# Gate stage of a RetNet and gated-MLP step: low part of v by VectorE a step later, gating chain cut into steps

## The chip, the cores and the metric

The kernel runs as one program on one core of a Trainium2 chip. The metric is the device time of an execution in microseconds (us). An execution is measured from its launch to its end. The profile shows one execution by itself, from the first to the last instruction (its span).

The core has a matrix engine (TensorE, PE in the rows; its weight loads are listed as PEld), a vector engine (VectorE, DVE), an activation engine (ScalarE, ACT), a general engine (GpSimd, POOL) and a queue processor (SyncE, SP) that here only issues DMAs. Each engine works through its own queue in order. An instruction that waits holds back all that stand behind it in that queue.

## The reference, cut to what matters

The model has two layers over 1024 prompt rows and 8 single new tokens (T = 1032 columns together), model width 1024. Layer 0 is a retention mixer; layer 1 is the chunked gated MLP that the change touches:

```python
u, v, g = split(x @ w_in, 3)             # each 2048 wide
u = gelu(u); v = layer_norm(gelu(v), ln_g, ln_b)
ws = where(causal, w_s[:, :128, :128], 0)        # 8 groups, 128 x 128
mixed = einsum('gij,bcjgd->bcigd', ws, chunks(v)) + b_s
y = u * mixed * silu(g)
x = layer_norm(ALPHA * x + y @ w_out)
```

All is fp32. The kernel gets near-fp32 products out of TensorE by splitting each operand into a high part (a cast to fp32r) and a low part (the value less the high part) and adding three products: high x high, high x low, low x high (`mm3`).

## The kernel before, in words

**Stages.** Layer 0 fills the first 950 us or so. Then `x1_transpose` and its sums prepare layer 1's input, units `tm34`, `tm36`, `tm38` compute v, and sixteen units `fm40` to `fm55` (class `FmUnit`, number n = 0 to 15) compute u and g, 128 columns of each per unit. This last stretch, from about 1135 to 1540 us, is the gate stage. An output projection (`OutProj`) ends the kernel.

**One unit.** A unit computes a 2 x 2 block product in seven products (`p5, p1, p3, p6, p2, p7, p4`), each in two steps (two column halves, c = 0 and 1, of 258 columns), so a unit is 14 steps. The order is written out by hand: the unit's `p5` stands ahead of the previous unit's `p4`, so steps 0 and 1 of a unit are its own `p5`, steps 2 and 3 are `p4` of the unit before, then come `p1`, `p3`, `p6`, `p2`, `p7`. Products of one unit accumulate in the same PSUM banks: `p6` goes on top of `p1`, so it can start only when ACT has copied `p1` out (`act.copy(t, ps)`, L1189); `p7` waits until DVE has added `p6`'s sum (L1193); `p3` waits for the copy of `p5`. Results lie in two tiles of 128 x 1032 per unit, `u` and `s`.

**Around each step**, the loop over `seq` calls `hook(s)`, which runs what was put on the list `later` (`run_later`) and then the prepared weight parts of coming products (`prep`: high part by ACT, L1164; low part by DVE, L1036, or for `p3`, `p2`, `p7` by a negation on ACT, L1167, and an accumulating DMA from POOL, L1171). Then it calls `hook_c2` (the spatial part, below), then the unit's step with its matmuls and evacuations. What is put on `later` in one step is issued at the head of the next.

**The end of a unit.** After `p4`'s second half, `later` gets `out`: in the next step (step 4 of the following unit) ACT makes the gelu of half of `u` (L1200) and, for even n, the silu of all of `s` (L1202); a step later (step 5) DVE multiplies `u` by `s` (L1203). For odd n the silu of `s` (L1197) runs one step after `p7`.

**The spatial part.** Group g (0 to 7) covers the two units 40+2g and 41+2g. `s_load` fetches gelu(v) from DRAM in two halves (`lv`, 128 x 4 x 256) with gain, bias and spatial weights (`gbw`). `s_prep` normalizes it, one quarter of a half per call (L1340, L1341 on DVE); part 0 first masks and splits the weights (POOL L1329, ACT `wsh` L1333, DVE `wsl` L1334). After each fourth part the half is split: `vh` by ACT's cast (L1345), `vl` by ACT's negation (L1346) and POOL's accumulating DMA that adds `lv` to it (L1347). From group 2 on, parts 0 to 3 are called in steps 4, 6, 8 and 10 of an odd unit and parts 4 to 7 in steps 0, 2, 4 and 6 of the next; groups 0 and 1 are prepared earlier, in `fm40` to `fm42`. `s_mix` (twelve matmuls `mx`, six for each half, which need both `vh` and `vl` of that half) stands at step 2 of an odd unit, for group 0 at step 0 of `fm42`. `s_y` transposes the result (PE `yt`, L1371) and multiplies it by `u` (DVE `yy`, L1374) at step 7 of the following units; the very first stands at step 4 of `fm42`.

**Other work in the stage.** `vd_norm` (DVE L1287, L1288, then `md` L1294) normalizes the new tokens' v, at step 2 of `fm41` and of `fm44`; `vdg` and `vdb` are its gain and bias tiles.

**Buffers.** Nearly every tile (`wr`, `w_p`, `wt`, `u`, `s`, `lv`, `gbw`, `vh`, `vl`, `mx`, `yy`, `vdg`, `vdb`, the operands made from layer 1's input) is one of `S(...)`: they share one pool of 49 buffers (`NSLOT`). A buffer is given on when all uses of its old tile are over; the first writer of a new tile then waits for the last user of the old one, whatever that was.

Of the kernel before, what the change touches and what calls it, by code (L numbers as in the profile page):

```python
# [13 lines left out]
AF = mybir.ActivationFunctionType  # L14
ALU = mybir.AluOpType
# [6 lines left out]
T = SEQ + NB  # L22
# [12 lines left out]
HT = T // 2  # L35
# [6 lines left out]
def retnet_gmlp_step(ctx: ExitStack, tc: tile.TileContext, a, o):  # L42
    nc = tc.nc
    act, dve, pool, pe, sp = nc.scalar, nc.vector, nc.gpsimd, nc.tensor, nc.sync
# [8 lines left out]
    def S(name, shape=(128, T), dt=F32):  # L53
        return big.tile(list(shape), dt, tag="s", name=name)

    def PS(name):
        return psp.tile([128, 512], F32, tag="ps", name=name)

    def f(ap):
        return ap.bitcast(F32)  # L60
# [4 lines left out]
    def mm3(out, lh, ll, rh, rl, start, stop, skip=False):  # L65
        mm(out, lh, rh, start, False, skip)
        mm(out, lh, rl, False, False, skip)
        mm(out, ll, rh, False, stop, skip)
# [70 lines left out]
    later = []  # L139
# [655 lines left out]
    def x_op(key, kt, sl):  # L795

        hh, ll = X[key]
        return hh[kt // 2][:, kt % 2, sl], ll[kt // 2][:, kt % 2, sl]
# [239 lines left out]
    class TmUnit(Unit):  # L1038
# [30 lines left out]
        def step(self, k, i):  # L1069
            ch, first = BANK[k], k in self.FIRST  # L1070
            if first and i % 2 == 0:
                self.ps[ch, i // 2] = PS(f"tm{self.p}{ch}_{i // 2}")
            ps = self.ps[ch, i // 2]
            wh, wl = self.op[k]
            sl = slice(i * 128, i * 128 + 128)
            out = ps[:, (i % 2) * 256:(i % 2) * 256 + 256]
            for kt in range(4):
                ws = slice(kt * 256, kt * 256 + 256)
                mm3(out, *x_op(XKEY[k], kt, sl), wh[:, ws], wl[:, ws], first and kt == 0 and i % 2 == 0, kt == 3,
                    skip=not first or i % 2 == 1)  # L1080
            if i % 2:
                self.evac(k, i // 2, ps)
            if i == 3:
                self.dec(k)
# [49 lines left out]
    class FmUnit(Unit):  # L1134
# [38 lines left out]
        def step(self, k, c):  # L1173
            ch, first = BANK[k], k in self.FIRST
            if first:
                self.ps[ch, c] = PS(f"fm{self.p}{ch}_{c}")
            ps = self.ps[ch, c][:, :258]
            wh, wl = self.op[k]
            sl = slice(c * 258, c * 258 + 258)
            for kt in range(4):  # L1180
                ws = slice(kt * 128, kt * 128 + 128)
                mm3(ps, wh[:, ws], wl[:, ws], *x_op(XKEY[k], kt, sl), first and kt == 0, kt == 3, skip=not first)
            i, n = OUT[k]
            if k == "p5":
                if c == 0:
                    self.q = [S(f"{s}{self.n}") for s in "us"]
            t = self.q[n][:, i * HT + c * 258:i * HT + c * 258 + 258]
            if k in ("p5", "p1", "p3"):
                act.copy(t, ps)  # L1189
            elif k == "p4":  # L1190
                act.activation(t, ps, AF.Gelu)
            else:
                dve.tensor_tensor(t, t, ps, ALU.add)  # L1193
            if c == 1:
                u, s = self.q
                if k == "p7" and self.n % 2:
                    later.append(lambda: act.activation(s, s, AF.Silu))  # L1197
                if k == "p4":
                    def out():
                        act.activation(u[:, :HT], u[:, :HT], AF.Gelu)  # L1200
                        if self.n % 2 == 0:
                            act.activation(s, s, AF.Silu)  # L1202
                        later.append(lambda: dve.tensor_tensor(u, u, s, ALU.mult))  # L1203
                    later.append(out)

    X1_SUMS = {}
    for n, (key, part) in {10: ("s1", 0), 11: ("s1", 3), 13: ("s1", 2), 14: ("s1", 5), 15: ("s2", 0), 16: ("s2", 3),
# [114 lines left out]
    def s_prep(g, part):  # L1322

        if g >= GR:
            return
        q = G[g]
        if part == 0:
            wr = q["wr"]
            pool.affine_select(out=wr, in_=wr, pattern=[[1, 128]], compare_op=ALU.is_ge, fill=0.0, base=0,  # L1329
                               channel_multiplier=-1)  # L1330
            wh = small.tile([128, 128], F32R, tag="wsh", name=f"wsh{g}")
            wl = small.tile([128, 128], F32R, tag="wsl", name=f"wsl{g}")
            act.copy(wh, wr)  # L1333
            dve.tensor_tensor(wl, wr, f(wh), ALU.subtract)  # L1334
            q["w"] = (wh, wl)
            q["vhl"] = []
        half, k = divmod(part, 4)
        t = q["v"][half]
        tb = half * 4 + k
        dve.scalar_tensor_tensor(t[:, k, :], t[:, k, :], vmv[:, tb, 0:1], q["gt"], ALU.subtract, ALU.mult)  # L1340
        dve.scalar_tensor_tensor(t[:, k, :], t[:, k, :], vrs[:, tb:tb + 1], q["bt"], ALU.mult, ALU.add)  # L1341
        if k == 3:
            hh = S(f"vh{g}_{half}", (128, 4, 256), F32R)
            ll = S(f"vl{g}_{half}", (128, 4, 256), F32R)
            act.copy(hh, t)  # L1345
            act.mul(ll, t, -1.0)  # L1346
            pool.dma_start(ll, t, accum_op=ALU.add)  # L1347
            q["vhl"].append((hh, ll))

    def s_mix(g):  # L1350
# [45 lines left out]
    def hook_c2(fb, o):  # L1396
# [15 lines left out]
        if (fb, o) in PREP0:  # L1412
            s_prep(0, PREP0.index((fb, o)))
        if (fb, o) in PREP1:
            s_prep(1, PREP1.index((fb, o)))
        if g == 0:
            if (fb, o) == (1, 5):
                s_load(1)
        elif odd:
            if o == 0:  # L1420
                s_load(g + 1)
            if o == 2:
                s_mix(g)
            if o in (4, 6, 8, 10):
                s_prep(g + 1, (o - 4) // 2)
        elif g > 1 and o in (0, 2, 4, 6):
            s_prep(g, 4 + o // 2)
# [25 lines left out]
    for u, k in seq:  # L1453
        for i in range(u.STEPS):
            s = first[u, k] + i
# [95 lines left out]
```

## Time and profile before

| | us |
|---|---|
| median of 3 runs | 1748.51 (1746.86 to 1751.27) |
| profiled execution | 1749.73 |
| its span, first to last instruction | 1748.0 |
| granted TensorE clock, mean over the span | 0.987 of full |
| busy in the span: PE / DVE / ACT / POOL | 1692.2 / 900.0 / 664.9 / 407.5 |

Busy times are sums over instructions of one engine. An idle stretch of an engine is put down to what released the instruction behind it ("<-"). A matmul's row gives when it started and, in brackets, how long PE had been idle before.

### The profile page before, as it was taken

What the parts mean: (1) busy time and instruction counts of PE and PEld (TensorE: products, weight loads), DVE (VectorE), ACT (ScalarE), POOL (GpSimd) and SP (SyncE); (2) the same over time, 40 slices, a digit from 0 to 9 for tenths busy, and PEclk for the clock granted to TensorE, in tenths of its full rate; (3) what the DMA queues carried; (4) which work ended last, traced back from release to release, by engine and by line L of the source; (5) the groups of instructions that cost most, each with busy time, mean ns of one, the idle gap of its engine ahead of it and who ended that gap; (6) DMA issues with size and microseconds to landing.
All of it is one profiled execution on the core that took longest, in us unless ns stands there. A gap on an engine that the chain in (4) does not pass through costs nothing. (4 is left out here: it accounts for less than half of the span.)

```text
span 1748.0 us, 25438 instructions
## 1 busy us (share of the span) xinstructions
PE 1692.2 (97%) x10304; PEld 1511.5 (86%) x10304; DVE 900.0 (51%) x1446; ACT 664.9 (38%) x1043; POOL 407.5 (23%) x331
## 2 busy tenths in 40 slices
PE   9999999999999999999999999997899999999996
PEld 8898897979999887877778999996889999977775
DVE  7134453633331577753359574564465555543347
ACT  4122424234332454431205343344556666731102
POOL 4122231411110666531107100011111111231103
PEclk9999999999999999999999999998999999999998
DMA  7135555555532544341102312263655666692206
GB/s 266 72 122 191 183 204 187 212 165 209 217 145 93 197 157 157 133 181 49 49 25 110 110 73 97 84 178 78 152 147 151 157 164 157 152 324 89 82 1 171
DMA packets 103174, 248.76 MB, mean 142 GB/s; under 512 B 9264, under 2 KB 37824, under 8 KB 103056
## 3 DMA queue, kind: packets, MB, share of 16 engines
q1 hardware_dynamic: 92736, 222.78, 36.5%
q0 software_dynamic: 10112, 24.15, 7.8%
q8 instruction: 81, 1.33, 0.3%
q14 instruction: 37, 0.30, 0.0%
q10 hardware_dynamic: 208, 0.20, 0.0%
HBM read 152.83 MB, written 69.93 MB: 127 GB/s over the span
## 5 line engine op out<-in xcount | busy, mean ns | idle before, releaser
L63 PE MATMUL fm<-xl,wh 128*128 128x344 f32 x768 | 246.6, 321 | 1.2 <-DVE xl L301 0.8
L63 PE MATMUL fm<-xh,wh 128*128 128x344 f32 x768 | 246.4, 321 | 1.3 <-ACT xh L300 1.3
L63 PE MATMUL fm<-xh,wl 128*128 128x344 f32 x768 | 246.1, 320 | 0.0
L63 PE MATMUL op<-wh,yh 128*128 128x512 f32 x512 | 202.4, 395 | 0.0
L63 PE MATMUL op<-wl,yh 128*128 128x512 f32 x512 | 201.7, 394 | 0.0
L63 PE MATMUL op<-wh,yl 128*128 128x512 f32 x512 | 201.7, 394 | 0.0
L63 PEld LDWEIGHTS fm<-xh,wh 128*128 128x128 f32 x768 | 144.9, 189 | 5.6 <-ACT xh L300 2.0
L63 PEld LDWEIGHTS fm<-xl,wh 128*128 128x128 f32 x768 | 144.7, 188 | 3.0 <-DVE xl L301 1.3
L63 PEld LDWEIGHTS fm<-xh,wl 128*128 128x128 f32 x768 | 144.7, 188 | 0.0
L130 ACT CAST wh<-wr 128x1024 fp32r<-128x1024 f32 x83 | 86.0, 1047 | 143.0 <-PE pd L63 58.9
L665 DVE TENSOR_TENSOR pre<-pre,op 128x512 f32<-128x512 f32 x96 | 65.7, 684 | 141.4 <-PE op L63 141.4
L134 DVE TENSOR_TENSOR wl<-wr,wh 128x1024 fp32r<-128x1024 f32 x77 | 107.6, 1403 | 46.2 <-ACT wh L130 28.6
L412 DVE SCALAR_TENSOR_TENSOR dw<-s,qd_dec,dw 128x512 f32<-128x512 f32 x32 | 40.0, 1251 | 170.1 <-ACT dw L411 170.1
L63 PEld LDWEIGHTS op<-wh,yh 128*128 128x128 f32 x512 | 96.1, 188 | 23.8
L63 PEld LDWEIGHTS op<-wh,yl 128*128 128x128 f32 x512 | 96.1, 188 | 22.7
L63 PEld LDWEIGHTS op<-wl,yh 128*128 128x128 f32 x512 | 96.2, 188 | 22.2
L63 PE MATMUL tm<-wl,xh 128*128 128x512 f32 x256 | 101.1, 395 | 0.0
L63 PE MATMUL tm<-wh,xl 128*128 128x512 f32 x256 | 100.9, 394 | 0.0
L63 PE MATMUL tm<-wh,xh 128*128 128x512 f32 x256 | 100.9, 394 | 0.0
L420 POOL TENSOR_TENSOR dhl<-dw,dhl 128x512 fp32r<-128x512 f32 x32 | 43.3, 1353 | 242.3 <-ACT dhl L419 234.4
L355 ACT ACTIVATE v<-tm,gneg 128x512 f32<-128x512 f32 x32 | 22.0, 689 | 202.3 <-PE tm L63 184.6
L1171 POOL DMA_DIRECT2D w_p<-wr x32 | 28.6, 895 | 295.8 <-PE tm38a L63 169.6
(829 smaller groups left out, 4262.4 us busy)
## 6 DMA issues: line engine op xcount, KB each, us to landing
wr<-in_w SPq DMA_DIRECT2D x127, 512.0 KB
s<-in_state SPq DMA_DIRECT2D x32, 512.0 KB
out_rs<-s SPq DMA_DIRECT2D x32, 512.0 KB
y_s<-yy SPq DMA_DIRECT2D x17, 512.0 KB
qk_s<-ro SPq DMA_DIRECT2D x16, 512.0 KB
v_s<-v SPq DMA_DIRECT2D x16, 512.0 KB
vbc<-vd_s SPq DMA_DIRECT2D x16, 512.0 KB
g_s<-g SPq DMA_DIRECT2D x16, 512.0 KB
```

Source lines behind the costliest of these rows:

```text
L63: pe.matmul(out, lhs, rhs, start=start, stop=stop, skip_group_check=skip)
L130: act.copy(t, src)
L134: eng.tensor_tensor(t, src, f(W[p][half][0]), ALU.subtract)
L355: act.activation(t[:, i % 2, :], ps, AF.Copy, scale=gneg[:, 2 * h + i % 2:2 * h + i % 2 + 1])
L412: dve.scalar_tensor_tensor(w[:, 0, :], s[:, 0, :], qd_dec[:, h, 0, b:b + 1], w[:, 1, :], ALU.mult, ALU.add)
L420: pool.tensor_tensor(hl[:, 1, :], w, f(hl[:, 0, :]), ALU.subtract)
L665: dve.tensor_tensor(dst, dst, ps, ALU.add)
L1171: pool.dma_start(self.op[k][1], src, accum_op=ALU.add)
```

## The change

The low part `vl` of a normalized half is no longer made by ACT's negation and POOL's DMA but by one DVE subtraction `lv - vh` (128 x 1024), issued at the head of the next step. The chain at a unit's end is cut up: the silu of `s` becomes two instructions of half the width, and the instructions of the chain are issued one per step. For even n that is: gelu half in step 4, silu halves in steps 5 and 6, product in step 7; before, gelu and silu in step 4, product in step 5. For odd n the silu halves stand in the two steps after `p7` (steps 0 and 1 of the next unit), the gelu and product where they were. The gelu was of a half already and the product stays one instruction.

```diff
             if c == 1:
                 u, s = self.q
+                lo, hi = slice(0, HT), slice(HT, T)
+                todo = []
                 if k == "p7" and self.n % 2:
-                    later.append(lambda: act.activation(s, s, AF.Silu))
+                    todo = [lambda: act.activation(s[:, lo], s[:, lo], AF.Silu),
+                            lambda: act.activation(s[:, hi], s[:, hi], AF.Silu)]
                 if k == "p4":
-                    def out():
-                        act.activation(u[:, :HT], u[:, :HT], AF.Gelu)
-                        if self.n % 2 == 0:
-                            act.activation(s, s, AF.Silu)
-                        later.append(lambda: dve.tensor_tensor(u, u, s, ALU.mult))
-                    later.append(out)
+                    todo = [lambda: act.activation(u[:, lo], u[:, lo], AF.Gelu)]
+                    if self.n % 2 == 0:
+                        todo += [lambda: act.activation(s[:, lo], s[:, lo], AF.Silu),
+                                 lambda: act.activation(s[:, hi], s[:, hi], AF.Silu)]
+                    todo.append(lambda: dve.tensor_tensor(u, u, s, ALU.mult))
+
+                def chain():
+                    if todo:
+                        todo.pop(0)()
+                        later.append(chain)
+                later.append(chain)
...
             act.copy(hh, t)
-            act.mul(ll, t, -1.0)
-            pool.dma_start(ll, t, accum_op=ALU.add)
+            later.append(lambda: dve.tensor_tensor(ll, t, f(hh), ALU.subtract))
             q["vhl"].append((hh, ll))
```

## Rows read from the trace of the kernel before

**Rows 1.** The page's busy times, us (share of the span) and instructions.
```profile
PE 1692.2 (97%) x10304; PEld 1511.5 (86%) x10304; DVE 900.0 (51%) x1446; ACT 664.9 (38%) x1043; POOL 407.5 (23%) x331
```
**Rows 2.** Windows, fm41 to fm47: length, busy by engine (x instructions), granted clock, DMA.
```profile
1159.51:1194.99 35.48, 27.58 (x190) 25.37 (x189) 21.49 (x43) 16.65 (x29) 4.64 (x6) 0.91 0.59 134
1194.99:1228.46 33.47, 27.41 (x185) 25.57 (x184) 14.97 (x33) 13.23 (x24) 2.59 (x3) 0.85 0.28 77
1228.46:1258.64 30.18, 25.82 (x191) 24.48 (x189) 13.97 (x31) 16.34 (x30) 3.77 (x5) 0.94 0.54 136
1258.64:1284.60 25.96, 23.68 (x186) 23.33 (x185) 17.77 (x36) 14.68 (x27) 4.94 (x6) 0.93 0.58 133
1284.60:1310.06 25.46, 24.05 (x190) 23.32 (x189) 13.16 (x29) 13.67 (x26) 2.27 (x4) 1.00 0.66 169
1310.06:1331.11 21.05, 21.05 (x179) 21.05 (x177) 14.11 (x30) 14.56 (x26) 5.19 (x6) 1.00 0.72 176
1331.11:1354.97 23.86, 23.86 (x191) 23.33 (x189) 13.16 (x29) 13.59 (x26) 2.04 (x3) 1.00 0.48 138
```
**Rows 3.** Timeline of PE: start, length, instruction, [idle before, releaser].
```profile
1173.50 0.39 PE L63 MATMUL fm41a<-xs2h,w_p 128*128 128x258 f32 x1 [2.02 <-ACT u L1189]
...
1192.69 0.79 PE L63 MATMUL mx<-vl,wsh 128*128 128x512 f32 x1 [4.72 <-DMA vl<-lv]
...
1213.95 1.12 PE L1371 MATMUL yt<-ident,mx 128*128 128x128 f32 x4 [3.15 <-ACT u L1191]
...
1236.28 0.79 PE L63 MATMUL mx<-vl,wsh 128*128 128x512 f32 x1 [3.15 <-DMA vl<-lv]
...
1255.66 0.39 PE L63 MATMUL fm43a<-xs3h,w_p 128*128 128x258 f32 x1 [1.22 <-DVE s L1193]
...
1269.72 0.39 PE L63 MATMUL fm44c<-xs4h,w_p 128*128 128x258 f32 x1 [2.28 <-ACT s L1189]
...
1307.07 0.39 PE L63 MATMUL fm45a<-xs3h,w_p 128*128 128x258 f32 x1 [1.41 <-DVE s L1193]
```
**Rows 4.** Instructions by line: ns min/median/max, first and last start; one DMA landing row.
```profile
L1346 ACT ACTIVATE vl<-lv x16: 1051/1056/1063, 1168.4 to 1501.8; 128x1024 fp32r<-128x1024 f32 x16
...
DMA to landing us min/median/max: 4.5/6.1/8.8
...
L134 DVE TENSOR_TENSOR wl<-wr,wh x54: 1203/1222/1954, 110.7 to 972.4; 128x1024 fp32r<-128x1024 f32 x54
...
L1202 ACT ACT_TABLE_LOAD  x8: 1283/1283/1283, 1170.8 to 1520.6; - x8
L1202 ACT ACTIVATE s<-s x8: 1063/1067/1069, 1172.1 to 1521.9; 128x1032 f32<-128x1032 f32 x8
```
**Rows 5.** Timelines of DVE and ACT, fm41 before its p6.
```profile
1164.77 1.27 DVE L1287 SCALAR_TENSOR_TENSOR vd<-vd,vdmv,vdg 8x1024 f32<-8x1024 f32 x1
1166.08 1.27 DVE L1288 SCALAR_TENSOR_TENSOR vd<-vd,vdrs,vdb 8x1024 f32<-8x1024 f32 x1
1171.03 1.37 DVE L1294 TENSOR_SCALAR md<-vd,w,b 8x256 f32<-8x256 f32 x4 [3.68 <-DMA w_p<-wt]
...
1166.07 0.38 ACT L1189 COPY s<-fm41c 128x258 f32<-128x258 f32 x1
...
1167.38 1.05 ACT L1345 CAST vh<-lv 128x1024 fp32r<-128x1024 f32 x1 [0.40 <-DVE vd L1288]
```
**Rows 6.** Timelines of DVE and ACT around mx of group 0 and step 4 of fm43.
```profile
1187.04 0.76 DVE L1036 TENSOR_TENSOR w_p<-wr,w_p 128x512 fp32r<-128x512 f32 x1 [2.12 <-ACT w_p L1164]
...
1247.00 0.29 DVE L1334 TENSOR_TENSOR wsl<-gbw,wsh 128x128 fp32r<-128x128 f32 x1 [13.93 <-ACT wsh L1333]
...
1184.33 1.05 ACT L1345 CAST vh<-lv 128x1024 fp32r<-128x1024 f32 x1 [0.66 <-ACT w_p L1167]
```
**Rows 7.** Timeline of ACT, fm42 and fm44.
```profile
1212.57 1.06 ACT L1346 ACTIVATE vl<-lv 128x1024 fp32r<-128x1024 f32 x1 [0.64 <-DMA w_p<-wt]
...
1266.73 0.62 ACT L1164 CAST w_p<-wr 128x512 fp32r<-128x512 f32 x1 [5.22 <-DMA vl<-lv]
```

## The prediction, made before the change was timed

> **What bounds the kernel now.** I read the page's busy times first: PE is busy 97% of the span and no other engine above 51% [rows 1]. So the change can only pay where PE stands still or runs slowly. Then the windows, one per gate unit. The reader is to see two regimes. `fm46` and `fm47` take 21.05 and 23.86 us with PE busy all the time at full clock; the even and odd units after them repeat these lengths. Nothing that ACT, DVE or POOL do there can shorten them. `fm41` to `fm45` do the same matmuls to within a few transposes and take 35.48, 33.47, 30.18, 25.96 and 25.46 us, so 36.9 us more than three odd and two even calm units (113.7). PE is idle for 7.90, 6.06, 4.36, 2.28 and 1.41 us of them, 22.0 together, and the granted clock is 0.91, 0.85, 0.94, 0.93 and 1.00. The clock costs about PE's busy time times what is missing: 2.5, 4.1, 1.5, 1.7 and 0 us, 9.8 together. What is to be had is thus some 32 us, all between 1160 and 1310 us.
>
> The timeline of PE says what ended the idle [rows 3]: twice the landing of `vl` (4.72 in `fm41`, for group 0; 3.15 in `fm43`, for group 1), three times an ACT evacuation (2.02, 3.15, 2.28), twice DVE's add of `p6` that `p7` waits for (1.22, 1.41). These seven are 17.95 of the 22.0 us.
>
> A third thing must be seen: the 49 shared buffers are used up here. In `fm41` DVE's `md` waits 3.68 us for a DMA into `w_p`, which it neither reads nor writes; ACT's copy of `s` starts at 1166.07, 0.03 us after `vd` L1287 ends, and `vh` at 1167.38, 0.03 us after L1288 ends, though neither touches `vd` [rows 5]. Each waits for a buffer that the other instruction gives back. In `fm44` ACT waits 5.22 us to write a weight part until the DMA from `lv` to `vl` is over [rows 7], a wait for `lv`'s buffer.
>
> **The change part by part.**
>
> *ACT.* Sixteen negations of 1.06 us go, 16.9 us [rows 4]. Eight even silus of 1.07 us become sixteen halves, at the same table loads of 1.28 us. In calm units that is worth nothing: PE waits for none of it. In `fm42` the negation at 1212.57 stands between the two gelu evacuations whose second one PE awaits at 1213.95 [rows 3, 7]: 1.06 us gained, taken as 1.1. Ends: all of that wait and the unit's clock part, 3.15 + 4.1 = 7.2 gained; below, 3 lost, two steps of 1.5 us (21.05/14), by which `s` now keeps its buffer longer.
>
> *POOL and the queues.* Sixteen DMAs of 512 KB go, with 4.5 to 8.8 us from issue to landing [rows 4], and POOL's weight DMAs no longer queue behind them. SP's queue keeps its order.
>
> *DVE.* Sixteen subtractions of 128x1024 are added. The same shape and operation takes 1.22 us as median on DVE (L134) [rows 4], 19.5 us in all, about 2.4 per pair of units. DVE is busy 27.3 of 44.9 us in a calm pair [rows 2], so it goes to about 66%. The subtraction waits for `vh` on ACT, which is issued one step before. Behind it stand, in odd units (step 11), the adds of `p2` and `p7`, in even units (step 7) the first product with `yt` and then `p6`'s add. PE needs these adds some three steps (4.5 us) later. So I cost it at nothing in calm units; if that cover were gone, up to 1.2 us a unit in ten units, 12 us, a rare case that the chances hold with the third rival.
>
> *The two vl waits.* For group 0, `vh` starts at 1184.33 and ends at 1185.4; DVE then idles 2.12 us until 1187.04 [rows 6], so the subtraction is done by about 1186.7, well before PE resumes at 1192.69. The 4.72 us go, with their share of `fm41`'s clock part (2.5 x 4.72/7.90 = 1.5): 6.2 gained. For group 1 the same holds: 3.15.
>
> *A new wait in fm41.* Here the change turns an order round. The subtraction of group 0's first half comes at the head of step 2 of `fm41`, ahead of L1287 and L1288 in DVE's queue, and waits for `vh`. But the buffer that `vh` takes now is the one that L1288 gives back. It has to be another. The next release that the rows show is the POOL DMA for which `md` waits until 1171.03. Then `vh` starts 3.7 us later than 1167.38. On ACT the second copy of `p5` (which lets `p3` go) stands behind it: 3.7 - 1.06 = 2.6 us later. On DVE: `vh` to 1172.1, subtraction to 1173.4, L1287, L1288 and `md` 3.9 us more, 1177.3 in place of 1172.4, 5 us late, and the adds that `p7` waits for come behind. PE loses between 2.6 and 5; I take 5, since in the two later odd units shown the same adds come late too [rows 3]. Ends: 0, if a free buffer is found, and 10, if the releases are awaited one after the other. Net for `fm41`: 6.2 - 5 = 1.2 gained, from 3.8 lost to 6.2 gained.
>
> *The silu out of step 4.* In `fm43` DVE stands 13.93 us before `wsl` because ACT's `wsh` comes late [rows 6]; in step 4 `wsh` is queued behind the gelu, a table load and the silu. The last two (2.35 us) move behind it, more than the 1.22 that PE then waits for `p6`'s add. The product moves from step 5 to 7, but stays ahead of the same adds. So all of `fm43`'s 4.36 idle goes, with its clock part 1.5: 5.9 gained; lower end 2, if only half of the `vl` wait is kept.
>
> *fm44 and fm45.* DVE's subtraction ends some 7 us before the DMA did, `lv`'s buffer comes back early, ACT's 5.22 us wait [rows 7] goes and with it the 2.28 behind it on PE, plus clock 1.7: 3.9 (low end 0). In `fm45` DVE's lead covers the 1.41: 1.4 (low end 0).
>
> **Sum.** 1.2 + 1.1 + 5.9 + 3.9 + 1.4 = 13.5 us off the profiled execution's 1749.73 us: 1736.2. The runs' median, 1748.51, lies 1.2 below that execution, so 1735. The rest of the 32 us stays: `fm41` and `fm42` still wait for buffers.
>
> **The rivals.**
>
> *A: buffers set the pace, and the kernel gets slower.* The price is in `fm41` to `fm43`: `s` of `fm40` and `fm42` is held two steps longer (3.0 us), which I charge once in each of the three units, 9 us; `fm41` loses its 10 against 6.2; only `fm44` and `fm45` gain (5.3). Net 9 + 3.8 - 5.3 = 7.5 lost: 1756. It decides as soon as the new buffer waits exceed the 18.5 us of removed waits (6.2 + 1.1 + 5.9 + 5.3). For it: [rows 5, 7]. Against it: `vl` and `lv` themselves are given back 5 us sooner. Of the pages, the Trainium skill's "Perfetto Trace Analysis", section "Optimization Strategy", bears on it: repeated gaps on the engine that should be saturated can mean that no memory is left for the next tile. The trace agrees for `fm41` and `fm42`; for `fm46` on there are no gaps.
>
> *B: the next wait takes the place.* Half of what `fm43` to `fm45` gain (11.2/2 = 5.6) goes to other ACT or DVE lateness, `fm41` loses 3.8, `fm42` gives nothing: 1.8 gained, 1747. For it: PE's waits have five different releasers in 150 us [rows 3]. Against it: the removed waits head the chains of the others in `fm43` and `fm44`.
>
> *C: the new wait in fm41 costs nothing.* Then 6.2 + 7.2 + 5.9 + 3.9 + 1.4 = 24.6 gained, 1724. For it: `fm41` has DVE idle for 14 of 35 us [rows 2]. Against: the order of the queues above.
>
> **How the numbers follow.** Forecast 0.50 (its own range 1728 to 1742), A 0.13, B 0.20, C 0.17. A measurement here can tell about 0.3%, 5.2 us, from no change. The forecast and C are faster by more; B is within it but for a rest on either side; A is slower. So faster 0.68, the same 0.19, slower 0.13. The range from 1722 to 1751 holds C, the forecast and nearly all of B.
>
> **What would show it.** In the changed profile: no PE wait on a DMA of `vl`; `fm41` still 33 to 36 us long, with a wait of PE on ACT's copy of `s` or on DVE in its `p3` or `p7` that is longer than before; `fm43` within 1 us of 23.86, `fm44` of 21.7; `fm46` on unchanged, with DVE some 2.4 us busier per pair of units and PE not waiting for it. Wrong if `fm42` to `fm44` keep idle PE with ACT or DVE waiting for tiles that they don't use, or if calm units get longer.

## The result, and the profile after

Over four runs each, side by side, the changed kernel takes 1739.37 us as median (1736.93 to 1741.81), the kernel before 1748.34 (1746.86 to 1751.27). The ratio is 0.9947, with a 95% interval of 0.9927 to 0.9966: 9.0 us faster, against a forecast of 13.3 and inside the range. One execution of the later kernel e3_vd_first took 3341.74 us and stands in no ratio below. The profiled execution of the changed kernel takes 1736.93 us, 12.8 less than the one before. Of these 12.8, 1.3 come before the gate stage and 0.9 after `fm45`, no more than single executions differ by (`fm40` starts between 1134.0 and 1137.8 us in the twelve traces of this case); 10.6 are won in `fm41` to `fm45`, where the prediction had 13.5.

The busy times of the page after, to set beside [rows 1]:

```profile
PE 1685.1 (97%) x10304; PEld 1506.2 (87%) x10304; DVE 918.1 (53%) x1462; ACT 654.8 (38%) x1045; POOL 393.4 (23%) x315
```

DVE is 18.1 us busier for its sixteen subtractions. ACT has lost only 10.1: the sixteen negations (16.9 us) went, but two silu halves take 1.26 us where a whole silu took 1.06, and two table loads came on top. PE still bounds the kernel: DVE goes from 51% to 53% of the span.

The windows of `fm41` to `fm47` after, with the columns of [rows 2] (length, busy by engine, granted clock, DMA):

```profile
1158.22:1196.65 38.43, 27.75 (x190) 25.94 (x189) 21.39 (x40) 14.03 (x27) 2.11 (x4) 0.87 0.29 74
1196.65:1227.21 30.56, 25.10 (x186) 23.56 (x184) 18.54 (x40) 12.78 (x24) 2.52 (x3) 0.94 0.32 96
1227.21:1251.42 24.21, 24.11 (x191) 23.37 (x189) 14.47 (x31) 15.67 (x30) 2.89 (x4) 1.00 0.54 144
1251.42:1274.28 22.86, 22.04 (x187) 21.67 (x186) 20.64 (x39) 12.90 (x26) 2.59 (x3) 1.00 0.50 127
1274.28:1298.16 23.88, 23.88 (x191) 23.35 (x190) 12.59 (x28) 13.68 (x28) 2.89 (x4) 1.00 0.55 142
1298.16:1319.13 20.97, 20.97 (x179) 20.97 (x177) 16.98 (x33) 12.67 (x25) 2.72 (x4) 1.00 0.50 138
1319.13:1342.97 23.84, 23.84 (x191) 23.31 (x189) 14.56 (x30) 15.26 (x29) 3.59 (x5) 1.00 0.62 164
```

| unit | before | after | predicted gain | measured gain |
|---|---|---|---|---|
| `fm41` | 35.48 | 38.43 | 1.2 | -2.95 |
| `fm42` | 33.47 | 30.56 | 1.1 | 2.9 |
| `fm43` | 30.18 | 24.21 | 5.9 | 6.0 |
| `fm44` | 25.96 | 22.86 | 3.9 | 3.1 |
| `fm45` | 25.46 | 23.88 | 1.4 | 1.6 |
| sum | | | 13.5 | 10.6 |

`fm43` and `fm45` are now calm units; `fm41` alone has grown. PE's timeline after answers to [rows 3] (start, length, instruction, idle before and its releaser):

```profile
1173.10 0.58 PE L63 MATMUL fm41c<-xs4h,w_p 128*128 128x258 f32 x1 [3.87 <-ACT s L1189]
1179.02 0.58 PE L63 MATMUL fm41a<-xs2h,w_p 128*128 128x258 f32 x1 [2.96 <-ACT u L1189]
1189.95 0.39 PE L63 MATMUL fm41a<-xs3h,w_p 128*128 128x258 f32 x1 [2.70 <-DVE s L1193]
...
1210.76 0.66 PE L1378 MATMUL yt<-ident,mx 128*128 128x128 f32 x4 [1.30 <-ACT u L1191]
1212.88 1.01 PE L1378 MATMUL yt<-ident,mx 128*128 128x128 f32 x4 [1.46 <-ACT u L1191]
1223.32 0.39 PE L63 MATMUL fm42a<-xs3h,w_p 128*128 128x258 f32 x1 [1.05 <-DVE s L1193]
...
1271.30 0.39 PE L63 MATMUL fm44a<-xs3h,w_p 128*128 128x258 f32 x1 [0.82 <-DVE s L1193]
```

No wait on a DMA of `vl` is left, and none of `fm43` and `fm45` is. In `fm41` three waits (3.87 in `p3`, 2.96 in `p6`, 2.70 in `p7`) have come in place of 2.02 (`p6`) and 4.72 (`vl`).

The timelines of ACT, POOL and DVE in `fm41` after, in order of time, show what is behind them; they answer to [rows 5] (lines have moved: `vh` L1353, `vl` L1354, `vd` L1295 and L1296, product L1206):

```profile
1167.10 0.37 ACT L1189 COPY s<-fm41c 128x258 f32<-128x258 f32 x1 [2.31 <-PE fm41a L63]
1167.37 0.64 ACT L1167 ACTIVATE w_p<-wt 128x512 fp32r<-128x512 f32 x1
1168.31 0.86 POOL L1171 DMA_DIRECT2D w_p<-wt  x1 [10.54 <-ACT w_p L1167]
1171.73 1.04 ACT L1353 CAST vh<-lv 128x1024 fp32r<-128x1024 f32 x1 [3.72 <-issue]
1172.68 0.37 ACT L1189 COPY s<-fm41c 128x258 f32<-128x258 f32 x1
1176.15 1.23 DVE L1354 TENSOR_TENSOR vl<-lv,vh 128x1024 fp32r<-128x1024 f32 x1 [12.59 <-PE fm41c L63]
1177.29 1.27 DVE L1295 SCALAR_TENSOR_TENSOR vd<-vd,vdmv,vdg 8x1024 f32<-8x1024 f32 x1
1178.59 0.37 ACT L1189 COPY u<-fm41a 128x258 f32<-128x258 f32 x1 [4.46 <-DVE vd L1295]
...
1186.70 0.62 ACT L1164 CAST w_p<-wt 128x512 fp32r<-128x512 f32 x1 [5.00 <-DVE u L1206]
```

This is a chain of buffers. Times are told here from the unit's start. The first copy of `s` starts at 8.88 instead of 6.56: in the kernel before it started 0.03 us behind `vd`'s first instruction, so its buffer came from there; that instruction now stands behind the subtraction. The weight part and its POOL DMA follow this copy and are later with it. `vh` starts at 13.51 instead of 7.87. The profile has no releaser for it, but that DMA, issued at 1168.31, lands after 3.3 us, that is at 1171.6, and `vh` starts at 1171.73. The issue row of that window (line, queue, KB, us to landing):

```profile
w_p<-wt POOLq DMA_DIRECT2D x1, 256.0 KB, 3.3
```

That this landing releases `vh` is thus read from the times, not shown by a row. The subtraction then has its operands at 1172.8 and starts only at 1176.15, 3.4 us later, when matmuls of `fm41c` end, which it doesn't read: its own output needs a buffer as well. `vd` starts at 19.07 instead of 5.26, and ACT's copy of `u`, for which PE stands in `p6`, waits 4.46 us for the buffer that `vd` gives back.

### The profile page after: what moved, and what is told of

It is laid out like the page before. It is cut to its first block, busy times and chain, and to the rows that moved or that the text cites. A ratio compares the mean times of both kernels' runs of the same rounds, so it can differ in the third digit from the quotient of the medians.

```text
span 1735.2 us, 25363 instructions
## 1 busy us (share of the span) xinstructions
PE 1685.1 (97%) x10304; PEld 1506.2 (87%) x10304; DVE 918.1 (53%) x1462; ACT 654.8 (38%) x1045; POOL 393.4 (23%) x315
## 5 line engine op out<-in xcount | busy, mean ns | idle before, releaser
L134 DVE TENSOR_TENSOR wl<-wr,wh 128x1024 fp32r<-128x1024 f32 x77 | 107.6, 1403 | 46.1 <-ACT wh L130 28.5
```

Of the source, the lines that this page charges most:

```text
L134: eng.tensor_tensor(t, src, f(W[p][half][0]), ALU.subtract)
```

## The experiments

The theory going in: the subtraction in place of the negation and the DMA gives most of the gain, the cut chain 2 to 4 us; and 7 to 11 us are lost in `fm41`, because the subtraction stands ahead of `vd_norm` in DVE's queue while the buffers that it needs come from behind it. The rivals: the loss comes from the cut chain, from too few buffers whatever the order, or from DVE's added work. Each kernel was timed in five rounds beside the kernel before.

**e1_vl_only: the new low part alone, on the kernel before.**

```diff
-            act.mul(ll, t, -1.0)
-            pool.dma_start(ll, t, accum_op=ALU.add)
+            later.append(lambda: dve.tensor_tensor(ll, t, f(hh), ALU.subtract))
```

> The kernel before with the low part of v by the DVE subtraction alone; the gating chain stays whole. Theory (two separate effects: the vl waits of fm42 to fm44 go through the subtraction, the late p6 adds of fm43 and fm45 through the silu's move): fm41 is as long as in the changed kernel or longer, 38 to 40 us, because the subtraction stands ahead of vd_norm in DVE's queue; no PE wait on a DMA of vl; fm43 about 25.5 (1.2 to 1.5 of wait for p6's add stays), fm45 about 25; time 3 to 7 us below before, ratio 0.996 to 0.998. Rival (the silu's move is what lets the rest gain): within 2 us of before.

Measured: 1739.92 us, ratio 0.9947 (0.9935 to 0.9959), the whole change's ratio. `fm41` to `fm45` take 36.65, 30.58, 25.32, 22.68 and 23.89 us. Two of the windows:

```profile
1160.14:1196.79 36.65, 27.73 (x191) 25.93 (x189) 21.34 (x40) 13.42 (x25) 2.10 (x4) 0.86 0.32 78
...
1227.37:1252.69 25.32, 24.08 (x191) 23.34 (x189) 14.42 (x31) 15.52 (x29) 2.90 (x4) 1.00 0.52 142
```

This part alone gains as much as the whole change. `fm41` loses 1.2 us by it, against 2.95 with the cut chain as well. The expectation missed twice: more was won than 3 to 7 us, and `fm41` is shorter than 38. Negation and DMA go together here, so the run doesn't tell what each was worth.

**e2_chain_only: the cut chain alone, with the negation and the DMA as before.** The edit is the first hunk of the change without the second.

> The kernel before with the cut-up gating chain alone; vl stays with ACT and the DMA. Theory: both PE waits on the DMA of vl stay (4 to 5 us in fm41, 3 in fm43), fm41 stays near 35.5, the waits for p6's add in fm43 and fm45 go, 2 to 4 us gained, ratio 0.998 to 0.999. Rival (the silu's move is the main part): 7 or more gained, ratio 0.996 or less. Rival (s held two steps longer in full buffers costs): slower by 2 us or more.

Measured: 1751.63 us, ratio 1.0007 (0.9995 to 1.0019): nothing, where 2 to 4 us were expected. Both `vl` waits are there (3.36 and 3.65 us). `fm43`'s wait for `p6`'s add went as expected, `fm45`'s stayed (1.21 us). And some calm units suffer: `fm47` takes 24.86 us, `fm53` 25.39. Its rows, POOL's, ACT's and PE's timeline and the window:

```profile
1341.28 0.29 POOL L1337 TENSOR_SCALAR_AFFINE_SELECT gbw<-gbw 128x128 f32<-128x128 f32 x1 [5.63 <-DMA gbw<-in_wsT]
1341.60 0.30 ACT L1341 CAST wsh<-gbw 128x128 fp32r<-128x128 f32 x1 [3.22 <-POOL gbw L1337]
1350.60 0.39 PE L63 MATMUL fm47a<-xs3h,w_p 128*128 128x258 f32 x1 [0.83 <-DVE s L1193]
...
1328.74:1353.60 24.86, 24.03 (x190) 23.31 (x189) 13.38 (x30) 13.51 (x27) 2.92 (x4) 1.00 0.60 168
```

ACT was free in time for `wsh`, but the spatial weights themselves were still being loaded. Taking the silu out of ACT's way bought nothing in this unit, because `gbw` wasn't there. POOL's instruction on it starts 12.5 us after the unit's start, in the changed kernel's `fm47` 9.0; why the load is later here wasn't followed.

**e3_vd_first: the changed kernel, with `vd_norm` a few instructions earlier, ahead of the subtraction on the list.**

```diff
-        if (fb, o) in ((1, 2), (4, 2)):
-            vd_norm(fb // 4)
+        if (fb, o) == (1, 1):
+            later.append(lambda: vd_norm(0))
+        if (fb, o) == (4, 2):
+            vd_norm(1)
```

> The changed kernel with one order turned back: vd_norm of fm41 is put on the list ahead of the subtraction, so that both come at the head of the same step 2 with vd_norm first on DVE. Nothing else moves. Theory (vh waits for a buffer that only vd_norm gives back, behind the subtraction): DVE's wait of 12.6 us before the first vl subtraction shrinks to under 4, fm41 goes from 38.4 to 27 to 31 us, the time 7 to 11 us below the changed kernel, ratio to before 0.988 to 0.991. Rival (buffers are used up anyway, the order doesn't matter): fm41 stays within 3 us of 38, ratio 0.993 to 0.996.

Measured: 1728.79 us, ratio 0.9884 (0.987 to 0.9898), 11 us below the changed kernel. `fm41` alone loses 10.4 us of its length: 38.43 to 28.05. Its window, and the timelines of ACT, DVE and PE:

```profile
1159.85:1187.90 28.05, 25.36 (x190) 24.42 (x189) 21.45 (x40) 14.03 (x27) 2.11 (x4) 0.94 0.42 101
...
1166.42 1.27 DVE L1296 SCALAR_TENSOR_TENSOR vd<-vd,vdrs,vdb 8x1024 f32<-8x1024 f32 x1
1167.73 1.05 ACT L1353 CAST vh<-lv 128x1024 fp32r<-128x1024 f32 x1 [0.40 <-DVE vd L1296]
1171.01 1.22 DVE L1354 TENSOR_TENSOR vl<-lv,vh 128x1024 fp32r<-128x1024 f32 x1 [0.94 <-DMA w_p<-wt]
...
1180.84 0.58 PE L63 MATMUL fm41a<-xs3h,w_p 128*128 128x258 f32 x1 [2.69 <-DVE s L1193]
```

`vh` starts 7.88 us after the unit's start, as in the kernel before, right behind the `vd` that gives back its buffer. The subtraction is through at 12.4 instead of 19.2. The waits in `p3` and `p6` are gone; that in `p7` stays. The theory holds.

**e4_slots50: the changed kernel with a 50th buffer.** A small tile (`y1d`) shares another's place (`yd`) to make room for it.

```diff
-NSLOT = 49
+NSLOT = 50
...
-    y1d = const.tile([128, 16, 16], F32R, name="y1d")
+    y1d = yd
```

> The changed kernel with 50 shared buffers in place of 49 (room is made by letting the second layer's small y1d tile share yd's place, whose use is over long before). Theory (buffers run out in fm41 and fm42): vh finds a buffer, fm41 shortens by 4 to 10 us and fm42 by 1 to 4, calm units stay at 21.0 and 23.8; ratio to before 0.986 to 0.992. Rival (only the order of the queues matters, or one buffer is taken by the next load at once): fm41 and fm42 within 2 us of 38.4 and 30.6, ratio 0.993 to 0.996.

Measured: 1734.92 us, ratio 0.9914 (0.9902 to 0.9926). `fm41` to `fm44` take 30.83, 27.49, 23.77 and 22.30 us, 11.7 less than in the changed kernel, so most of what was lost there were waits for buffers. But `fm40`, calm until then, goes from 24.21 to 28.88, and a buffer comes late there, as DVE's timeline shows (the instruction waits for matmuls of `fm40c`, which it doesn't read). That the 50th buffer does this by passing all buffers on in another order is argued, not shown:

```profile
1150.78 0.69 DVE L1154 TENSOR_TENSOR wt<-wr 128x512 f32<-128x512 f32 x1 [2.94 <-PE fm40c L63]
```

**e5_vl_vd: e1 and e3 together, so without the cut chain.**

> The subtraction with vd_norm ahead of it, but the gating chain whole as before. Theory (the chain's cut moves the product behind wt in fm41, which made p7 wait 2.7 us, and its gain of about 1.1 us in fm43 is smaller): fm41 26 to 27.5 us against 28.05 in the version with the cut chain, fm43 1 us longer than there, sum within 1.5 us of that version, ratio to before 0.987 to 0.990. Rival (the cut chain is needed once the vl waits are gone): 3 us or more slower than that version, ratio 0.990 or more.

Measured: 1728.85 us, ratio 0.9884 (0.9866 to 0.9902); `fm41` to `fm45` 26.95, 31.41, 25.31, 22.70 and 23.89. The cut chain adds nothing: with it `fm43` is 0.7 us shorter, `fm41` 1.1 longer.

**e6_vd_first50: e3 and e4 together.**

> The changed kernel with vd_norm ahead of the subtraction and 50 shared buffers. Theory (both mend the same wait of vh, and the 50th buffer also brings back a loss in fm40): the gains don't add; fm40 near 28.9 as with 50 buffers alone, fm41 26 to 29, fm42 27 to 28, ratio 0.989 to 0.991. Rival (two separate causes): the gains add, ratio 0.985 or less.

Measured: 1732.41 us, ratio 0.9898 (0.9879 to 0.9917). `fm41` takes 27.51 and `fm42` 27.18, 4 us less than in e3 the two together, but `fm40` 27.93, 3.8 more. The gains don't add up.

**e7_same_step: the subtraction right behind the cast, not a step later.**

```diff
-            later.append(lambda: dve.tensor_tensor(ll, t, f(hh), ALU.subtract))
+            dve.tensor_tensor(ll, t, f(hh), ALU.subtract)
```

> The changed kernel with the subtraction issued in the step of its cast, not at the head of the next. Theory (one step is only cover for ACT's 1.05 us): DVE idles about 1 us before each of the 16 subtractions, PE waits for none of it in calm units, fm41 stays at 37 to 40 us since the subtraction is still ahead of vd_norm; ratio to before 0.993 to 0.997. Rival (the step's delay is what keeps DVE's adds in time): calm units longer by 0.5 us or more, ratio 0.998 or more.

Measured: 1744.49 us, ratio 0.9976 (0.9963 to 0.9988), between the two. Calm units keep 21.1 and 23.85 us; `fm41` takes 40.87 and `fm43` 26.01. So the step of delay is worth some 5 us, in units where DVE is behind, and nothing in calm ones: PE waits 1.77 us (`fm41`, second half of `p7`; 0.63 in the changed kernel) and 1.58 us (`fm43`; none there) for DVE's adds. `fm41` is a little longer than the 37 to 40 us expected.

**e8_vd_first_before: the edit of e3 on the kernel before.**

> The kernel before with vd_norm of fm41 put on the list a step earlier (head of step 2, ahead of nothing new). Theory (the order of vd_norm matters only because the subtraction was put ahead of it): no change, ratio 0.9985 to 1.0015. Rival (vd_norm in itself comes too late in fm41): 3 us or more faster, ratio 0.998 or less.

Measured: 1748.02 us, ratio 0.9993 (0.9982 to 1.0005); `fm41` 35.34. An earlier `vd_norm` is worth nothing by itself: what e3 wins is what the subtraction ahead of it had lost.

**e9_double_sub: e3, with each subtraction issued twice.** The second repeats the first, into the same tile.

```diff
             later.append(lambda: dve.tensor_tensor(ll, t, f(hh), ALU.subtract))
+            later.append(lambda: dve.tensor_tensor(ll, t, f(hh), ALU.subtract))
```

> The version with vd_norm ahead of the subtraction, every subtraction issued twice (the same result twice). Theory (in calm units DVE has room for it): calm units stay at 21.0 and 23.8 us; fm41 to fm44, where DVE's adds are late already, lose up to 1.2 us each, so 0 to 5 us over the version with single subtractions (ratio to before 0.9884 to 0.991). Rival (DVE is near the limit in every unit): 0.5 us or more in each calm unit, 8 us or more in all, ratio 0.993 or more.

Measured: 1741.81 us, ratio 0.9953 (0.9934 to 0.9971), some 12 us above e3. `fm41`, `fm42` and `fm44` lose 1.5, 1.7 and 4.0; calm odd units keep 23.8 to 23.9. Of the calm even ones `fm46` keeps 21.06, and `fm48` to `fm54` go from 21.0 to between 22.3 and 23.2. `fm48`'s window and PE's timeline in it:

```profile
1343.21:1365.54 22.33, 21.45 (x178) 21.12 (x177) 18.39 (x35) 11.82 (x24) 2.58 (x3) 1.00 0.44 111
...
1362.55 0.39 PE L63 MATMUL fm48a<-xs3h,w_p 128*128 128x258 f32 x1 [0.88 <-DVE s L1193]
```

The theory missed here. In four of the five calm even units DVE's cover holds one subtraction and not a second, although DVE is busy for only 18.39 of 22.33 us in the first of them. Why `fm46` has room wasn't followed.

**e10_mixed: e3, with the chain of `fm40` (n = 0) as it was, so that `fm41` gets `s`'s buffer back early.**

```diff
-                if k == "p4":
+                if k == "p4" and self.n == 0:
+                    def out():
+                        act.activation(u[:, lo], u[:, lo], AF.Gelu)
+                        act.activation(s, s, AF.Silu)
+                        later.append(lambda: dve.tensor_tensor(u, u, s, ALU.mult))
+                    todo = [out]
+                elif k == "p4":
```

> The version with vd_norm ahead of the subtraction and the chain cut up in all units but n = 0, whose product in fm41 stays at step 5. Theory (the cut chain costs in fm41 and gains in fm43): fm41 27 us as with the whole chain, fm43 24.2 to 24.7 as with the cut one, 0.5 to 2 us below either, ratio 0.987 to 0.988, which may not be told from 0.9884. Rival (the waits only move on to fm42): no difference, 0.988 to 0.989.5 with fm42 longer by what fm41 gains.

Measured: 1728.57 us, ratio 0.9878 (0.9858 to 0.9897). `fm41` takes 26.97 us, `fm43` 23.95, as hoped, but `fm42` 31.29, 0.6 more than in e3. With e3 and e5 it beats both kernels, by some 20 us the one before; the three can't be told apart by these intervals.

## Why the prediction was right, and where its sizes were off

**Direction, place and mechanism were right.** The gain lies in `fm41` to `fm45`, comes from the subtraction in place of negation and DMA (e1 against e2), and is cut by the turned order in `fm41` (e3). The calm units didn't move. Only `fm41` itself went the other way: 1.2 gained was forecast, 2.95 lost was measured.

**The new wait in fm41 is the mis-sized term.** The prediction had 5 us, with 10 as its end "if the releases are awaited one after the other". e3 took away 10.4 us: 8.0 of PE standing still (10.68 us idle against 2.69) and 2.4 of PE running slower (busy 27.75 against 25.36 us for the same 190 matmuls, clock 0.87 against 0.94). So that end was nearly exact, but only with a clock part that the term didn't have. The prediction followed one buffer, that of `vh`, to its next release. There were two more: the copy of `s` ahead of `vh` on ACT also drew its buffer from `vd` (8.88 instead of 6.56 us, by which the POOL DMA itself came later), and `vl` needs one of its own, for which the wait now stands in DVE's queue, ahead of `vd_norm`. Both could be asked of [rows 5]: the copy of `s` starting 0.03 us behind L1287 stands there and was read, but not moved along. With 10 in place of 5 the sum is 8.5 us; measured are 9.0 between the medians and 10.6 in the windows. That it comes so near is in part luck: `fm42` and the `vl` wait gave more than their terms, `fm44` less, and no term held what the cut chain costs in `fm41` (all below). The rule weighed with rival A (the Trainium skill's "Perfetto Trace Analysis", section "Optimization Strategy": repeated gaps can mean that no memory is left for the next tile) agrees in kind with `fm41` after the change too: PE's gaps of 3.87 and 2.96 us stand behind waits for buffers on ACT and DVE, and a 50th buffer shortens the unit by 7.6 us (e4). But these gaps stand in one unit and don't repeat as the section has it, and the net loss that rival A made of it isn't there.

**The vl wait of group 0** was put at 6.2 with its clock share. With the new wait away (e3), `fm41` is 7.4 us shorter than before, and with the chain whole as well (e5) 8.5. In e5 PE is busy for 24.50 us instead of 27.58, at a clock of 1.00, so the clock's share was 3.1 and not 1.5. And some of what the stall cost lay in the next unit, as the clock shows. These windows are of the kernel before, with the columns of [rows 2], around the 4.72 us wait (granted clock third from the right):

```profile
1188.00:1192.69 4.69, 0.00 (x0) 0.00 (x0) 3.65 (x9) 2.41 (x4) 0.93 (x2) 0.89 0.97 200
1192.69:1195.00 2.31, 2.31 (x6) 1.82 (x7) 0.00 (x0) 0.20 (x1) 0.00 (x0) 0.50 0.99 229
1195.00:1200.00 5.00, 5.00 (x30) 5.00 (x29) 2.45 (x5) 1.32 (x3) 0.00 (x0) 0.65 0.18 74
```

After the change, the same place:

```profile
1193.00:1197.00 4.00, 4.00 (x24) 3.45 (x23) 3.81 (x8) 2.54 (x7) 0.43 (x1) 1.00 0.56 100
1197.00:1202.00 5.00, 5.00 (x44) 5.00 (x43) 4.15 (x10) 2.31 (x4) 0.45 (x1) 1.00 0.76 234
```

**fm42** was put at 1.1 and gave 2.9. After the stall PE ran at 0.50, the lower of its levels, for 2.31 us and at 0.65 in the mean of the next 5.00. The second stretch, 5.00 x 0.35 = 1.75 us, lies in `fm42`, whose clock part the prediction left out of its value and held in the upper end. It is won back with the stall. PE's wait behind the negation fell from 3.15 to 1.46, by 1.7 instead of the 1.06 of the negation, but 0.78 became 1.30 and `p7`'s 0.59 became 1.05: together 0.7 gained there. The larger part of the 2.9 is PE's busy time, 27.41 to 25.10.

**fm43** was right to 0.1 us, and so was its reason in kind: e1 keeps a 1.24 us wait for `p6`'s add ([rows 3] has 1.22) and a length of 25.32; with the cut chain it is 24.21. So the chain is worth 1.1 there. In calm odd units, too, `wsh` now starts right behind the gelu, as ACT's timeline in `fm47` shows:

```profile
1328.16 0.63 ACT L1202 ACTIVATE u<-u 128x516 f32<-128x516 f32 x1
1328.68 0.29 ACT L1341 CAST wsh<-gbw 128x128 fp32r<-128x128 f32 x1
```

That the product's move to step 7 costs nothing was wrong in `fm41`. It now ends `s`'s use later, behind `wt` in DVE's queue. DVE's timeline after the change, and DVE's and ACT's in e1:

```profile
1184.23 0.69 DVE L1154 TENSOR_TENSOR wt<-wr 128x512 f32<-128x512 f32 x1 [1.14 <-PE md L1308]
...
1185.45 1.22 DVE L1206 TENSOR_TENSOR u<-u,s 128x1032 f32<-128x1032 f32 x1
...
1186.08 0.68 DVE L1154 TENSOR_TENSOR wt<-wr 128x512 f32<-128x512 f32 x1
1186.88 0.62 ACT L1164 CAST w_p<-wt 128x512 fp32r<-128x512 f32 x1 [5.72 <-DVE wt L1154]
```

ACT's weight part reads this `wt`. In e1 it starts 0.1 us behind it; after the change it starts at 1186.70, 1.8 us behind it, when the product ends (the last row of the `fm41` timelines above), though it doesn't read the product: a wait for a buffer again. ACT's idle time before it is no measure of this: 5.00 us, and 5.72 in e1. `p7` waits 2.70 us, in e1 0.95, and `fm41` is 1.8 us longer than in e1. What the chain gives in `fm43` it loses in `fm41`, so its halves are worth nothing (e1, e5). This is rival A's mechanism, at a fifth of its 9 us. The Trainium skill's "Perfetto Trace Analysis", section "Optimizing Scalar/DVE Operations", says that breaking up instructions may let work end sooner where an engine isn't saturated and yet causes gaps on another. ACT is such an engine here (38% busy). In `fm43` it gained 1.1 us; in all the runs show no gain from it, since e1 and the whole change are both at 0.9947.

**fm44 and fm45**, put at 3.9 and 1.4, gave 3.1 and 1.6. e1 has both at full (22.68 and 23.89), so it was the subtraction and not the cut chain; `fm45` stays at 25.9 to 26.0 where the DMA stays (e2, e8). For `fm44` this is less clear: with the DMA it also comes down, to 23.40 (e2) and 23.78 (e8), where ACT waits 4.64 and 4.26 us for that DMA and not 5.22. `fm44`'s 2.28 us wait is gone; 0.82 behind DVE's add is left.

**DVE's work at nothing** was right for one subtraction, which takes the 1.22 us that L134 gave. But e9 shows how little was left. The prediction compared 66% with 100%; by `fm48`'s row in e9 what decided was how much fits ahead of `p6`'s add in an even unit.

Of the signs announced: no wait on `vl`, `fm43` within 1 us of 23.86 (24.21), unchanged calm units and DVE some 2 us busier per pair (15.0 + 14.5 = 29.5 in `fm48` and `fm49`, against 27.3) came as told. `fm41` was to take 33 to 36 us and took 38.43; `fm44`, at 22.86, missed its 1 us around 21.7 narrowly. One sign of being wrong is there in part: `fm42` keeps 5.46 us of idle PE, and ACT's copy of `s` there waits 3.47 us for matmuls of `fm42a`, which it doesn't read. That wait was the same before the change (3.47), and the prediction's sum left it in place.

## What to carry to other kernels

Before an instruction goes to the head of an in-order queue, list every tile that it and the instruction it waits for must write, and ask which instruction gives back that buffer: if it is one behind it in the same queue, the order has been turned round, and the price is the whole chain of later releases, here 10.4 us in one unit for a 1.22 us instruction. Follow all the writers on the path, not only the first; here, with the pool full, the upper end was the right one. Put the instructions that give buffers back ahead of those that take them, before cutting up anything that is off the path.

## What the runs showed that was not expected

One buffer more is not simply better: it took 11.7 us off `fm41` to `fm44` and put 4.7 on `fm40`. The second subtraction cost four of the five calm even units 1.3 to 2.1 us, more than the 1.22 us that it takes, with DVE busy for 82 to 83% of them. And the clock's loss outlives the wait behind it: 4.69 us of standstill were followed by 2.31 us at 0.50 and 5.00 us at 0.65, 2.9 us by these rows, of which 1.75 fell in the next unit.
